# A two-layer decoder trunk on one core: the token order of the group products, the mean of a layer norm, and the last stores

## The chip, the cores and the metric

The kernel runs on 1 core of one Trainium2 chip. The metric is device time in microseconds (us) of that core, the median over several runs. TensorE (PE in the profile; PEld is its weight load) multiplies matrices into PSUM, which has eight banks of 128 partitions x 512 float32 each. VectorE (DVE) and ScalarE (ACT) do the elementwise work, GpSimd (POOL) and SyncE (SP) issue transfers; ACT can issue them too.

## The reference, cut to what matters

All tensors are float32; `x` is (1, 256, 2048): 256 tokens with 2048 features. Layer 0 mixes tokens by pooling, layer 1 by a dilated attention whose keys and values come from the stream behind layer 0; each is followed by a convolutional FFN of inner width 5504, and each of the four sublayers by `layer_norm(alpha * h + mix)`.

```python
def pool_mixer(h, w_in, w_grp, scale, w_out):
    p = (h @ w_in).reshape(B_, S, 4, 512)
    ...                       # pooled: per group a trailing mean over 2, 4, 8 or 16 tokens, minus p
    mixed = jnp.einsum('bsgc,gcd->bsgd', pooled, w_grp).reshape(B_, S, D) * scale
    return mixed @ w_out

def layer_norm(x, g, b):
    mu = jnp.mean(xf, axis=-1, keepdims=True)
    var = jnp.mean(jnp.square(xf - mu), axis=-1, keepdims=True)
    return (xf - mu) * lax.rsqrt(var + 1e-5) * g + b

for i in range(2):
    mix = pool_mixer(...) if i == 0 else dilated_attention(h, h0 @ shared_w_k, h0 @ shared_w_v, ...)
    h = layer_norm(ALPHA * h + mix, ln1_g[i], ln1_b[i])
    h = layer_norm(ALPHA * h + conv_ffn(h, ...), ln2_g[i], ln2_b[i])
```

## The kernel before, in words

**Units.** All weights are read once, in blocks of 512 rows by 512 columns (1 MB), and each block is a unit: it is loaded (`do_load`, line 61, SP's queue, three buffers), split into a high part rounded to PE's float32r format and the rest (`do_split`, lines 86 and 87: `wh` by ACT, then `wl` by DVE, four buffers each), and multiplied. `run_units` (line 105) goes through the units in the order of the list. For unit i it first emits the loads up to i + 5 and the splits up to i + 3 (`ahead`), then the functions put down for this unit in `before`, then the unit's matmuls, then the functions that `later(n, ...)` put off and that are due, then the unit's own evacuation (`post`). This is the order of the instructions on every engine, and each engine works off its own in order. The split of unit i + 3 writes the buffers that unit i - 1 read.

**Operands.** The stream is kept with features on partitions, in "quads": tiles of 128 partitions x 4 blocks x (high, low) x 256 tokens (`quad_tile`, 263). Every product is summed from three: high x high, high weight x low stream, low weight x high stream. `mm_quad` (147) makes such a unit with the weights as the held operand and the tokens as the moving one: 16 pairs of a row block k and a column block m. In mode "ab" a pair is a matmul of 512 columns (L186) and one of 256 (L188); in modes "a", "x" and "grp" it is three of 256 or 258 (L190, L191, L192). In a group's last unit m is the outer loop. The tokens are moved through PE by `cols` (159). The usual order is `twine` (129): the two halves of the 256 tokens in turn (token 0, token 128, token 1, ...); `untwine` and `phi` (132, 141) read a bank back. Four banks hold the results of a group of units (`group`, 197).

**Token order.** From the first layer's residual on, the stream keeps the 128 tokens of a half in another order, j-major with token = 4k + j (j = 0 to 3, k = 0 to 31). The input product and the pooling work in natural order. The new order comes in at the four group products (`add_grp`, 543, mode "grp", one unit each): there `cols` reads `pooled` as `p j k a`, so the results come out in the new order. `grp_post` (505) scales them and writes `mixed`, high part by ACT (L511), low part by DVE (L512). Units of the first layer: the input product for group 3, then group 2, the group product of 3, input 1, group product 2, input 0, group product 1, two units of the output product, group product 0, the other fourteen. An input group is four units, and its evacuation (`pool_post`, 474) does the pooling on DVE; its last step, `lo_part` (L267), ends `pooled`.

**The mean.** `chain` (395) makes the layer norm of a finished residual: PE sums the stream and its squares over the features into one bank (`ps[0]`, L399), the mean in columns 0 to 255 and the mean square behind it. L404 squares the mean (ACT), L405 subtracts (DVE), `root` takes the root (L408, ACT), its reciprocal (L409) and mean times reciprocal (L410, both DVE). It is called three times. With `which` 0 (both first norms) `root` follows at once. With `which` 1 (the end of layer 0) it is put off to the next unit, behind that unit's split. What follows, over the next units: `norm` (L420, L421), `affine` (L427, L429: the high part `xc`) and `lo` (L267: the low part). PE meanwhile works on the unnormalised stream `xp` (mode "x"): behind layer 0 on the first key group (4 units) and the first query group (4 units). The value product (`group_tm`, 215, with `tm_block`, 206, L211 to L213) then reads `xc`; there the tokens are held, a unit is 24 matmuls of 512 columns, and the third of them is the first to read the low part.

**The end.** The last down projection works by token rows, so the last norm goes by rows of 128 tokens (t = 0, t = 1). `finish_second` (807) writes the last four column blocks with L832, in the order 0, 1, 3, 2, and calls `store` (748) behind each: four transfers of 32 partitions x 2 KB, as the tokens' order asks. For t = 1 they go in turn to SP and ACT.

Of the kernel before, what the change touches and what calls it, by code (L numbers as in the profile page):

```python
# [9 lines left out]
F32 = mybir.dt.float32  # L10
F32R = mybir.dt.float32r
I32 = mybir.dt.int32
AF = mybir.ActivationFunctionType
OP = mybir.AluOpType
# [3 lines left out]
T = 256  # L18
# [15 lines left out]
def trunk(ctx: ExitStack, tc: tile.TileContext, x, pool_w_in, pool_w_grp, pool_scale, pool_w_out,  # L34
          attn_w_q, attn_w_o, shared_w_k, shared_w_v, ffn_w_up, ffn_conv_w, ffn_conv_b, ffn_w_down,
          ln1_g, ln1_b, ln2_g, ln2_b, out):
    nc = tc.nc
    V, A, PE = nc.vector, nc.scalar, nc.tensor
# [10 lines left out]
    def bank(nm):  # L49
        return psp.tile([P, 512], F32, name=nm, tag="ps")  # L50
# [22 lines left out]
    def do_split(i, n=4):  # L73
        if i not in parts:
            r = raw.pop(i)
            shape = [P, r.shape[1], r.shape[2]]
            if i < len(units) - 2:
                wh[i] = wp.tile(shape, F32R, name=f"wh{i}", tag="wh")
                wl[i] = wp.tile(shape, F32R, name=f"wl{i}", tag="wl")
            else:  # L80
                for w, nm in ((wh, "wxh"), (wl, "wxl")):
                    v = quad_tile(nm).rearrange("p k l c -> p (k l c)")[:, :shape[1] * shape[2]]
                    w[i] = v.rearrange("p (k n) -> p k n", n=shape[2])
            parts[i] = [(r[:, s], wh[i][:, s], wl[i][:, s]) for s in pieces(i, r.shape[1])]
        for r, h, l in parts[i][:n]:
            A.copy(h, r)  # L86
            V.tensor_tensor(l, r, h.bitcast(F32), OP.subtract)  # L87
        parts[i] = parts[i][n:]
# [40 lines left out]
    def twine(w):  # L129
        return w.rearrange("p (a c) -> p c a", a=2)  # L130

    def untwine(ps):
        return ps.rearrange("p (c a) -> p a c", a=2)

    def apart2(v):
        return v.rearrange("p (a c) -> p a c", a=2)
# [4 lines left out]
    def phi(ps):  # L141
        return untwine(ps[:, :T])
# [4 lines left out]
    def mm_quad(xq, ps, first, last, mode, mid):  # L147
        def go(h, l):
            nk, nb = h.shape[1], h.shape[2] // P
            order = [(k, m) for k in range(nk) for m in range(nb)]  # L150
            if last:
                order = [(k, m) for m in range(nb) for k in range(nk)]
            if first:
                for m in range(nb):
                    ps.append(bank("acc"))
            q = xq()
            n = XW if mode == "x" else T

            def cols(k, j):
                if mode == "grp":  # L160
                    return q[:, k, j, :n].rearrange("p (a k j) -> p j k a", a=2, j=4)
                return twine(q[:, k, j, :n])

            u = state["done"]
            if u < 2:
                for k in range(nk):
                    if k == 3 - u:
                        if u == 0:
                            x_quad(1, (0,))
                            do_split(1, 1)  # L170
                            x_quad(1, (1,))
                            do_split(1, 1)
                        else:
                            mid()
                    for w, j, st in ((h, 0, first and k == 0), (h, 1, False), (l, 0, False)):
                        for m in range(nb):
                            PE.matmul(ps[m][:, :n], w[:, k, m * P:(m + 1) * P], cols(k, j), start=st, stop=False)  # L177
                        if u == 0 and k == 1 and j == 0 and w is h:
                            x_quad(0, (1,))
                            do_split(0, 2)  # L180
                return
            for i, (k, m) in enumerate(order):
                c = slice(m * P, (m + 1) * P)
                st, sp = first and k == 0, last and k == nk - 1
                if mode == "ab":
                    PE.matmul(ps[m], h[:, k, c], q[:, k, :, :T].rearrange("p l (a c) -> p l c a", a=2),  # L186
                              start=st, stop=False)
                    PE.matmul(ps[m][:, :T], l[:, k, c], cols(k, 0), start=False, stop=sp)  # L188
                else:
                    PE.matmul(ps[m][:, :n], h[:, k, c], cols(k, 0), start=st, stop=False)  # L190
                    PE.matmul(ps[m][:, :n], h[:, k, c], cols(k, 1), start=False, stop=False)  # L191
                    PE.matmul(ps[m][:, :n], l[:, k, c], cols(k, 0), start=False, stop=sp)  # L192
                if mid is not None and i == 7:
                    mid()
        return go

    def group(w, r0s, c0, ncol, xqs, post, mode="ab", mids=()):
        ps = []
        for j, (r0, nr) in enumerate(r0s):
            last = j == len(r0s) - 1  # L200
            units.append((w[r0:r0 + nr, c0:c0 + ncol],
                          mm_quad(xqs[j], ps, j == 0, last, mode, mids[j] if j < len(mids) else None),
                          (lambda: post(ps)) if last else None))
# [59 lines left out]
    def quad_tile(nm):  # L263
        return xcp.tile([P, 4, 2, XW], F32R, name=nm, tag="xc")
# [130 lines left out]
    def chain(ps, lay, which, after):  # L395
        mean, msq = ps[:, :T], ps[:, T:]
        for o, v in ((mean, ST["S"]), (msq, ST["Q"])):
            for i in range(2):
                PE.matmul(o, invr, v[:, i], start=i == 0, stop=i == 1)  # L399
        t2 = lnp.tile([P, 2, T], F32, name="var", tag="fold2")  # L400
        rm = lnp.tile([P, 4, T], F32, name="rm", tag="sq")[:, 0:2]
        rs, mr = rm[:, 0:1, :], rm[:, 1:2, :]
        ST["rs"], ST["mr"] = rm[:, 0, :], rm[:, 1, :]
        A.activation(t2[:, 0, :], mean, AF.Square)  # L404
        V.tensor_tensor(t2[:, 1, :], msq, t2[:, 0, :], OP.subtract)  # L405

        def root():
            A.activation(t2[:, 1, :], t2[:, 1, :], AF.Sqrt, bias=epst)  # L408
            V.reciprocal(rm[:, 0, :], t2[:, 1, :])  # L409
            V.tensor_tensor(rm[:, 1, :], mean, rm[:, 0, :], OP.mult)  # L410

        if which == 0:
            root()
        else:
            before.setdefault(state["done"] + 1, []).append(root)
        mb, rb = mr.to_broadcast([P, 4, T]), rs.to_broadcast([P, 4, T])
        g0 = 32 * which

        def norm(q):
            V.tensor_tensor(H[q], H[q], rb, OP.mult)  # L420
            V.tensor_tensor(H[q], H[q], mb, OP.subtract)  # L421

        def affine(q):
            XC[q] = quad_tile("xc")
            for m in range(4):
                j = 4 * q + m
                A.activation(H[q][:, m, :], H[q][:, m, :], AF.Identity,  # L427
                             scale=vec[lay][:, g0 + j:g0 + j + 1], bias=vec[lay][:, g0 + 16 + j:g0 + 17 + j])
            A.copy(XC[q][:, :, 0, :T], H[q])  # L429

        def lo(q):
            lo_part(XC[q], H[q], 4)
            if after is not None:
                later((8, 11, 14, 19)[q], lambda: after(q))

        later(1, lambda: norm(0))
        for q in range(4):
            later(2 + q, lambda q=q: affine(q))
            if q < 3:
                later(2 + q, lambda q=q: norm(q + 1))  # L440
            later(3 + q, lambda q=q: lo(q))
# [30 lines left out]
    pooled_q, mixed_q = {}, {}  # L472
# [32 lines left out]
    def grp_post(g):  # L505
        def post(ps):
            mixed_q[g] = t = quad_tile("mixed")
            for m in range(4):
                sc = vec[0][:, 64 + 4 * g + m:65 + 4 * g + m]
                th, tl = apart2(t[:, m, 0, :T]), apart2(t[:, m, 1, :T])  # L510
                A.activation(th, phi(ps[m]), AF.Copy, scale=sc)  # L511
                V.scalar_tensor_tensor(tl, phi(ps[m]), sc, th.bitcast(F32),  # L512
                                       op0=OP.mult, op1=OP.subtract)
        return post

    XIN = {}
# [24 lines left out]
        group(pool_w_in[0], rows4, 512 * g, 512, xsrcs, pool_post(g), mode="ab" if g < 3 else "a", mids=mids)  # L541

    def add_grp(g):
        group(pool_w_grp[0, g], [(0, 512)], 0, 512, [lambda: pooled_q[g]], grp_post(g), mode="grp")

    marks = []
    add_in(3, mids=[None] + [lambda q=q: x_quad(q) for q in (2, 3)])
# [1 line left out]
    add_grp(3)  # L549
    add_in(1)  # L550
    add_grp(2)
    add_in(0)
    add_grp(1)
# [194 lines left out]
    def store(c, t):  # L748
        rows = out[0, t * P:(t + 1) * P, 512 * c:512 * c + 512].rearrange("(k j) c -> j k c", j=4)
        for j in range(4):  # L750
            queue = A if t == 1 and j % 2 == 1 else nc.sync
            queue.dma_start(rows[j], HT[c][32 * j:32 * j + 32, t, :])

    def tm_post(c, first, last, back=False):
# [85 lines left out]
    scale = 1.0 / math.sqrt(P)  # L840
# [162 lines left out]
    with tc.tile_pool(name="pool", bufs=1) as pp:  # L1003
# [5 lines left out]
        for l in range(2):  # L1009
            n = 80 if l == 0 else 64  # L1010
# [93 lines left out]
```

## Time and profile before

| what | value |
|---|---|
| median of 3 runs | 1944.86 us (1944.46 to 1946.63) |
| the profiled execution | 1945.11 us, its span 1942.9 us |
| mean granted PE clock | 0.999 |
| PE busy | 99% (10486 matmuls) |
| DVE, ACT, POOL busy | 72%, 51%, 16% |
| DMA | 409.89 MB, 211 GB/s |

The span runs from the first to the last instruction of the profiled execution; launch and end around it are in the execution's own time. A line of the timeline gives the start in us, the duration in us, the engine, the line of the code, the operation, what is written and read, and the count; in brackets stands the engine's idle time in front of it and what ended it. SPq, ACTq and POOLq are the queues on which these engines issue transfers. Matmuls are pipelined: a duration is longer than the distance from one start to the next, and the distance is what the matmul costs.

### The profile page before, as it was taken

How to read it: one execution, taken by the hardware profiler on the slowest of the kernel's cores; microseconds unless marked ns; L12 is line 12 of the kernel's file. 1: busy time of each engine (PE TensorE's matmuls, PEld its weight loads, DVE VectorE, ACT ScalarE, POOL GpSimd, SP SyncE). 2: the span in 40 equal slices, each digit the busy share in tenths (PEclk: the TensorE clock that was granted, in tenths of full speed). 3: DMA queues.
4: the chain of work that ended last, by engine and by line, in shares of the span. 5: the costliest groups of instructions: out<-in, count | busy, mean ns of one | idle time of the engine just before them, and what ended most of it. 6: DMA issues, size and time to landing. Idle time of an engine off the chain costs nothing.

```text
span 1942.9 us, 27350 instructions
## 1 busy us (share of the span) xinstructions
PE 1931.4 (99%) x10486; PEld 1733.4 (89%) x10486; DVE 1408.5 (72%) x1782; ACT 996.0 (51%) x1048; POOL 308.6 (16%) x599
## 2 busy tenths in 40 slices
PE   9999999999999999999999999999999999999998
PEld 9999998888888888999999999998888888888897
DVE  7757987856675676789877657888765675575677
ACT  6444575535543554555654444575544553553562
POOL 2000005502110116100033110003511110100100
PEclk9999999999999999999999999999999999999999
DMA  8644648966766667665575665647876665656655
GB/s 275 202 162 151 217 168 253 266 225 207 248 217 208 230 212 227 208 215 195 169 226 187 197 203 174 203 158 232 259 244 211 233 230 203 222 209 219 206 186 183
DMA packets 226018, 409.89 MB, mean 211 GB/s; under 512 B 20462, under 2 KB 39300, under 8 KB 225632
## 3 DMA queue, kind: packets, MB, share of 16 engines
q1 hardware_dynamic: 206912, 389.85, 60.3%
q0 software_dynamic: 18592, 17.78, 3.8%
q8 instruction: 82, 1.34, 0.3%
q10 hardware_dynamic: 384, 0.52, 0.1%
q14 instruction: 48, 0.39, 0.1%
HBM read 380.01 MB, written 2.10 MB: 197 GB/s over the span
## 4 chain that ended last, share of the span: by engine, by line
PE 97%; DVE 2%; DMA 0%; issue 0%; ACT 0%; SPq 0%; DVEq 0%
PE t L211 20%; PE t L213 20%; PE t L212 20%; PE acc L186 18%; PE acc L188 9%; PE acc L190 3%; PE acc L192 3%; PE acc L191 3%; DVE wl L87 1%; PE acc L177 1%; PE s L894 0%; PE o L953 0%; DVE xp L390 0%; DMA raw<-in_attn_w_q_dram 0%; DMA raw<-in_pool_w_in_dram 0%; DVE fold L329 0%
## 5 line engine op out<-in xcount | busy, mean ns | idle before, releaser
L87 DVE TENSOR_TENSOR wl<-raw,wh 128x2048 fp32r<-128x2048 f32 (+2 forms) x374 | 815.1, 2185 | 443.3 <-ACT wh L86 436.4
L86 ACT CAST wh<-raw 128x2048 fp32r<-128x2048 f32 (+2 forms) x374 | 679.8, 1824 | 639.6 <-PE t L213 372.2
L211 PE MATMUL t<-wh,xc 128*128 128x512 f32 x1184 | 449.6, 380 | 0.0
L212 PE MATMUL t<-wl,xc 128*128 128x512 f32 x1184 | 448.7, 379 | 0.0
L213 PE MATMUL t<-wh,xc 128*128 128x512 f32 x1184 | 448.7, 379 | 0.0
L186 PE MATMUL acc<-xc,wh 128*128 128x512 f32 x960 | 317.6, 384 | 0.0
L613 POOL DMA_DIRECT2D u<-b x264 | 130.0, 500 | 1127.8 <-DVE b L604 719.1
L188 PE MATMUL acc<-xc,wl 128*128 128x256 f32 x960 | 261.2, 272 | 0.0
L213 PEld LDWEIGHTS t<-wh,xc 128*128 128x128 f32 x1184 | 223.8, 189 | 31.8
L211 PEld LDWEIGHTS t<-wh,xc 128*128 128x128 f32 x1184 | 223.8, 189 | 31.7
L212 PEld LDWEIGHTS t<-wl,xc 128*128 128x128 f32 x1184 | 223.8, 189 | 31.6
L211 PE MATMUL t<-wh,g 128*128 128x512 f32 x590 | 222.8, 378 | 0.0
L212 PE MATMUL t<-wl,g 128*128 128x512 f32 x590 | 222.8, 378 | 0.0
L213 PE MATMUL t<-wh,g 128*128 128x512 f32 x590 | 222.8, 378 | 0.0
L186 PEld LDWEIGHTS acc<-xc,wh 128*128 128x128 f32 x960 | 180.6, 188 | 26.7 <-ACT h L537 0.6
L188 PEld LDWEIGHTS acc<-xc,wl 128*128 128x128 f32 x960 | 184.3, 192 | 0.4
L629 DVE SCALAR_TENSOR_TENSOR c<-u,cv,c 128x256 f32<-128x256 f32 x344 | 141.2, 479 | 5.9 <-ACT c L625 5.4
L211 PEld LDWEIGHTS t<-wh,g 128*128 128x128 f32 x590 | 111.5, 189 | 15.7
L213 PEld LDWEIGHTS t<-wh,g 128*128 128x128 f32 x590 | 111.5, 189 | 15.6
L212 PEld LDWEIGHTS t<-wl,g 128*128 128x128 f32 x590 | 111.5, 189 | 15.6
L190 PE MATMUL acc<-xp,wh 128*128 128x258 f32 x384 | 106.5, 277 | 4.2 <-DVE rm L410 4.2
L191 PE MATMUL acc<-xp,wh 128*128 128x258 f32 x384 | 106.4, 277 | 0.0
(222 smaller groups left out, 2348.5 us busy)
## 6 DMA issues: line engine op xcount, KB each, us to landing
raw<-in_ffn_w_up_dram SPq DMA_DIRECT2D x160, 1024.0 KB, 5.0
raw<-in_ffn_w_down_dram SPq DMA_DIRECT2D x80, 1024.0 KB, 5.6
raw<-in_pool_w_out_dram SPq DMA_DIRECT2D x16, 1024.0 KB, 5.1
raw<-in_shared_w_k_dram SPq DMA_DIRECT2D x16, 1024.0 KB, 5.2
raw<-in_attn_w_q_dram SPq DMA_DIRECT2D x16, 1024.0 KB, 5.3
raw<-in_shared_w_v_dram SPq DMA_DIRECT2D x16, 1024.0 KB, 5.7
raw<-in_attn_w_o_dram SPq DMA_DIRECT2D x16, 1024.0 KB, 5.2
raw<-in_pool_w_in_dram SPq DMA_DIRECT2D x12, 1024.0 KB, 5.8
```

Of the source, the lines that this page charges most:

```text
L86: A.copy(h, r)
L87: V.tensor_tensor(l, r, h.bitcast(F32), OP.subtract)
L186: PE.matmul(ps[m], h[:, k, c], q[:, k, :, :T].rearrange("p l (a c) -> p l c a", a=2), start=st, stop=False)
L188: PE.matmul(ps[m][:, :T], l[:, k, c], cols(k, 0), start=False, stop=sp)
L190: PE.matmul(ps[m][:, :n], h[:, k, c], cols(k, 0), start=st, stop=False)
L191: PE.matmul(ps[m][:, :n], h[:, k, c], cols(k, 1), start=False, stop=False)
L192: PE.matmul(ps[m][:, :n], l[:, k, c], cols(k, 0), start=False, stop=sp)
L211: PE.matmul(ps, xh, hk, start=first and k == 0, stop=False)
L212: PE.matmul(ps, xh, lk, start=False, stop=False)
L213: PE.matmul(ps, xl, hk, start=False, stop=last and k == nk - 1)
L613: queue.dma_start(w[32 * i:32 * i + 32, 2 + j, :], v[32 * j:32 * j + 32, i, :])
L629: V.scalar_tensor_tensor(c[:, :, m], u[:, i:i + 4, m], cv[:, i, j:j + 1], c[:, :, m], op0=OP.mult, op1=OP.add)
```

## The change

The moving operand of the group products is now `twine`, as elsewhere (their mode is "a"), so their results come out in natural order, and the new order is taken in the evacuation: ACT and DVE read the bank as `p a j k`, whose innermost step is eight floats, and write `mixed` in one run. DVE does each column block in two instructions, one for each half of the tokens. In `chain`, ACT copies the mean into the tile that will hold mean times reciprocal, and `root` multiplies there in place, so that L405 and this copy are the last readers of the bank. The last stores (t = 1) go to SP, SP or ACT by block, ACT, and GpSimd; those of t = 0 stay on SP.

```diff
--- before.py
+++ after.py
@@ -157,8 +157,6 @@
             n = XW if mode == "x" else T
 
             def cols(k, j):
-                if mode == "grp":
-                    return q[:, k, j, :n].rearrange("p (a k j) -> p j k a", a=2, j=4)
                 return twine(q[:, k, j, :n])
 
             u = state["done"]
@@ -402,12 +400,13 @@
         rs, mr = rm[:, 0:1, :], rm[:, 1:2, :]
         ST["rs"], ST["mr"] = rm[:, 0, :], rm[:, 1, :]
         A.activation(t2[:, 0, :], mean, AF.Square)
+        A.copy(rm[:, 1, :], mean)
         V.tensor_tensor(t2[:, 1, :], msq, t2[:, 0, :], OP.subtract)
 
         def root():
             A.activation(t2[:, 1, :], t2[:, 1, :], AF.Sqrt, bias=epst)
             V.reciprocal(rm[:, 0, :], t2[:, 1, :])
-            V.tensor_tensor(rm[:, 1, :], mean, rm[:, 0, :], OP.mult)
+            V.tensor_tensor(rm[:, 1, :], rm[:, 1, :], rm[:, 0, :], OP.mult)
 
         if which == 0:
             root()
@@ -507,10 +506,12 @@
             mixed_q[g] = t = quad_tile("mixed")
             for m in range(4):
                 sc = vec[0][:, 64 + 4 * g + m:65 + 4 * g + m]
-                th, tl = apart2(t[:, m, 0, :T]), apart2(t[:, m, 1, :T])
-                A.activation(th, phi(ps[m]), AF.Copy, scale=sc)
-                V.scalar_tensor_tensor(tl, phi(ps[m]), sc, th.bitcast(F32),
-                                       op0=OP.mult, op1=OP.subtract)
+                th, tl = (apart2(t[:, m, i, :T]).rearrange("p a (j k) -> p a j k", j=4) for i in range(2))
+                src = phi(ps[m]).rearrange("p a (k j) -> p a j k", j=4)
+                A.activation(th, src, AF.Copy, scale=sc)
+                for a in range(2):
+                    V.scalar_tensor_tensor(tl[:, a], src[:, a], sc, th[:, a].bitcast(F32),
+                                           op0=OP.mult, op1=OP.subtract)
         return post
 
     XIN = {}
@@ -541,7 +542,7 @@
         group(pool_w_in[0], rows4, 512 * g, 512, xsrcs, pool_post(g), mode="ab" if g < 3 else "a", mids=mids)
 
     def add_grp(g):
-        group(pool_w_grp[0, g], [(0, 512)], 0, 512, [lambda: pooled_q[g]], grp_post(g), mode="grp")
+        group(pool_w_grp[0, g], [(0, 512)], 0, 512, [lambda: pooled_q[g]], grp_post(g), mode="a")
 
     marks = []
     add_in(3, mids=[None] + [lambda q=q: x_quad(q) for q in (2, 3)])
@@ -748,7 +749,7 @@
     def store(c, t):
         rows = out[0, t * P:(t + 1) * P, 512 * c:512 * c + 512].rearrange("(k j) c -> j k c", j=4)
         for j in range(4):
-            queue = A if t == 1 and j % 2 == 1 else nc.sync
+            queue = nc.sync if t == 0 else (nc.sync, (nc.sync, A, A, nc.sync)[c], A, nc.gpsimd)[j]
             queue.dma_start(rows[j], HT[c][32 * j:32 * j + 32, t, :])
 
     def tm_post(c, first, last, back=False):
```

## The prediction

> **What bounds the kernel now.** I read the page first: its busy table, the chain that ended last, then the waits of TensorE (PE), and only then single stretches of the timeline.
>
> ```profile
> span 1942.9 us, 27350 instructions
> PE 1931.4 (99%) x10486; PEld 1733.4 (89%) x10486; DVE 1408.5 (72%) x1782; ACT 996.0 (51%) x1048; POOL 308.6 (16%) x599
> ```
>
> The longest wait of PE (us in total, times, longest; the next two in that view are of the warm-up, before 10 us, and about a microsecond each):
>
> ```profile
> PE acc L190 <- DVE rm L410: 4.2, 1, 4.2
> ```
>
> PE is busy for 99% of the span and waits once for long. So three things can change the end: how long PE needs for its matmuls, that one wait of 4.2 us, and the tail behind PE's last matmul. Each part of the change touches one of them. The profiled execution took 1945.11 us, of which 2.2 lie around the span; the median of the three runs is 1944.86, 0.25 less. I sum against the execution and carry the differences over to the median.
>
> **Part 1, the group products.** A busy PE says nothing about its pace, so I looked at starts. The four units that read `pooled` have 48 matmuls each. Starts and durations, for the first and the last of the four: its first matmul, then the first one behind it; in between stands the start of the second group unit, four ordinary units later:
>
> ```profile
> 54.55 0.39 PE L190 MATMUL acc<-pooled,wh 128*128 128x256 f32 x1
> ...
> 65.53 0.40 PE L186 MATMUL acc<-xc,wh 128*128 128x512 f32 x1
> ...
> 86.50 0.40 PE L190 MATMUL acc<-pooled,wh 128*128 128x256 f32 x1
> ...
> 139.92 0.40 PE L190 MATMUL acc<-pooled,wh 128*128 128x256 f32 x1
> ...
> 150.89 0.40 PE L186 MATMUL acc<-mixed,wh 128*128 128x512 f32 x1
> ```
>
> 10.98 and 10.97 us, 0.229 us a matmul; an ordinary unit takes (86.50 - 65.53) / 4 = 5.24. The new operand has the form of the `g` units of the last column block of layer 0's down projection: same 256 columns, same three matmuls, two halves in turn, one element a step. There are 132 of them:
>
> ```profile
> 881.72 0.28 PE L190 MATMUL acc<-g,wh 128*128 128x256 f32 x1
> ...
> 896.46 0.28 PE L190 MATMUL acc<-xp,wh 128*128 128x258 f32 x1
> ```
>
> 14.74 us / 132 = 0.1117 us. So the old operand, which walks tokens in steps of four (16 bytes), runs at half the pace. A unit becomes 48 x 0.1117 = 5.36 us, and four of them save 4 x (10.98 - 5.36) = **22.5 us** of PE time.
>
> Does PE get that time, or does it then wait? What lies around the first group unit, on VectorE (DVE):
>
> ```profile
> 54.79 2.29 DVE L87 TENSOR_TENSOR wl<-raw,wh 128x2048 fp32r<-128x2048 f32 x1 [1.72 <-ACT wh L86]
> ...
> 63.81 2.28 DVE L87 TENSOR_TENSOR wl<-raw,wh 128x2048 fp32r<-128x2048 f32 x1
> 66.02 1.22 DVE L267 TENSOR_TENSOR pooled<-po,pooled 128x1024 fp32r<-128x1024 f32 x1
> 67.15 1.66 DVE L512 SCALAR_TENSOR_TENSOR mixed<-acc,vec,mixed 128x256 fp32r<-128x256 f32 x4
> 68.72 2.28 DVE L87 TENSOR_TENSOR wl<-raw,wh 128x2048 fp32r<-128x2048 f32 x1
> ```
>
> Counted off in the program, these three splits are of the second, third and fourth unit behind the group unit. It will now end at 59.9, and those three start at 65.1, 70.4 and 75.6. Their splits end at 57.1, 66.1 and about 71.7 (below), a slack of 8, 4.3 and 3.9 us. The next group unit is due at 80.9; its operand, `pooled` above, is done at 67.2. The later groups are looser: there DVE idles ahead of most splits, because ACT waits for PE to free a weight buffer. Over the whole stage:
>
> ```profile
> 54.50:151.00 96.50, 96.50 (x515) 88.03 (x514) 60.03 (x60) 39.60 (x45) 0.00 (x0) 1.00 0.52 174
> ```
>
> DVE has 60.0 us of work in 96.5; with 22.5 less it has 60 to 62 in 74, 84%, and DMA stands at 0.52. PE stays the bound.
>
> The evacuation now reads the bank in steps of eight floats (32 bytes) and DVE does it in two halves. Nothing in the trace reads a bank so; the nearest rows are two ScalarE (ACT) copies of 512 columns, contiguous (L534) and in runs whose step is four floats (L537):
>
> ```profile
> L534 ACT CAST xc<-xT x7: 586/586/597, 4.7 to 23.8; 128x512 fp32r<-128x512 f32 x7
> L537 ACT COPY h<-xT x8: 581/604/618, 15.2 to 32.7; 128x512 f32<-128x512 f32 x8
> L512 DVE SCALAR_TENSOR_TENSOR mixed<-acc,vec,mixed x16: 475/478/485, 67.2 to 151.6; 128x256 fp32r<-128x256 f32 x16
> 972.33 0.28 DVE L910 SCALAR_TENSOR_TENSOR p<-p,cnt 128x128 f32<-128x128 f32 x1
> ```
>
> 604 against 586 ns: a step costs ACT 3% at most. Half the columns take DVE 0.28 us, so a pair 0.56 for 0.478; a group's evacuation grows by 4 x 0.08 = 0.3 us, or 0.7 at 0.33 a half. All of it lies in the slack of 3.9 us, so I cost it at nothing; between nothing and twice the old price (1.9 us a group) the sum is the same. From the other side: the Trainium skill's "SBUF — State Buffer", section "Door 1: The DMA port swizzle", says that PSUM has lines of 8 bytes and that any non-contiguous PSUM access slows matmuls significantly. It speaks of matmuls, and ACT's row at 16 bytes does not show it; whether it holds for DVE at 32 no row tells. I make it a rival below.
>
> **Part 2, the mean.** The one wait of PE, the row before it, and the clock after it (window: length, then busy us of PE, PEld, DVE, ACT, POOL, PE clock, DMA share, GB/s):
>
> ```profile
> 919.28 0.27 PE L192 MATMUL acc<-xp,wl 128*128 128x258 f32 x1
> 923.75 0.58 PE L190 MATMUL acc<-xp,wh 128*128 128x258 f32 x1 [4.20 <-DVE rm L410]
> ```
>
> ```profile
> 923.75:929.70 5.95, 5.95 (x40) 5.95 (x41) 5.88 (x5) 3.12 (x5) 0.00 (x0) 0.74 0.48 153
> ```
>
> PE should have gone on at 919.39, so it lost 4.36 us, and then ran at a mean clock of 0.74 for 5.95 us, 1.55 us more: 5.9 in all. What it waited for is the bank that holds the mean, of which L410 is the last reader:
>
> ```profile
> 917.08 0.42 DVE L405 TENSOR_TENSOR var<-acc,var 128x256 f32<-128x256 f32 x1
> 919.29 2.29 DVE L87 TENSOR_TENSOR wl<-raw,wh 128x2048 fp32r<-128x2048 f32 x1 [1.79 <-ACT wh L86]
> ...
> 923.28 0.42 DVE L410 TENSOR_TENSOR rm<-acc,rm 128x256 f32<-128x256 f32 x1
> ```
>
> With the copy the bank is free after L405, at 917.5, 1.9 us before PE needs it. The copy is at most 0.6 us of ACT (L537 above moves twice the columns in 0.604) in front of this:
>
> ```profile
> 917.35 1.90 ACT L86 CAST wh<-raw 128x2048 fp32r<-128x2048 f32 x1 [3.56 <-DMA raw<-in_attn_w_q_dram]
> ```
>
> ACT idles 3.56 us there, so the copy is free. Behind the copy are queued only the splits and the root. In the two other chains (near 235 and 1272) the root follows at once; ACT waits for L405 between square and root anyway, so the copy fits in, and no PE wait is there to be removed.
>
> What is late next? The chain of root, norm and affine on DVE and ACT stays, since it hangs on the weights that land at 917.35. PE will come earlier to the value product, which reads the new stream:
>
> ```profile
> 945.75 0.38 PE L211 MATMUL t<-wh,xc 128*128 128x512 f32 x1
> ...
> 946.18 0.38 PE L213 MATMUL t<-wh,xc 128*128 128x512 f32 x1
> ```
>
> ```profile
> 937.49 1.22 DVE L267 TENSOR_TENSOR xc<-h,xc 128x1024 fp32r<-128x1024 f32 x1
> ...
> 945.29 1.22 DVE L267 TENSOR_TENSOR xc<-h,xc 128x1024 fp32r<-128x1024 f32 x1
> ...
> 951.03 1.22 DVE L267 TENSOR_TENSOR xc<-h,xc 128x1024 fp32r<-128x1024 f32 x1
> ```
>
> ```profile
> 929.76 1.91 ACT L86 CAST wh<-raw 128x2048 fp32r<-128x2048 f32 x1 [0.48 <-PE acc L191]
> ```
>
> Two starts in 0.43 us are 0.215 us a matmul, 24 x 0.215 = 5.16 us a unit. Without the stall the product starts at 945.75 - 5.9 = 939.85. It needs the low parts of quads 0, 1, 2 from the third matmul (0.43 us) of each unit. DVE and ACT gain only the 0.48 us that ACT waits for PE at 929.76, so the low parts end at 938.2, 946.0 and 951.75. Quad 0 is in time; quad 1 is wanted at 945.44 and costs 0.6; quad 2 is then wanted at 951.2 and costs 0.5. So 1.1 of the 5.9 come back as small waits and **4.8 us** stay; 4.3 if DVE and ACT don't move at all, 5.9 if they move more.
>
> **Part 3, the last stores.** The last result of DVE, the last issues, the wait in front of them, and issues and landings by queue:
>
> ```profile
> 1937.43 0.74 DVE L832 SCALAR_TENSOR_TENSOR ht<-ht,mv,w 128x512 f32<-128x512 f32 x1
> ```
>
> ```profile
> 1939.23 0.82 SPq L752 DMA_DIRECT2D out_dram<-ht  x2
> 1939.45 0.79 ACTq L752 DMA_DIRECT2D out_dram<-ht  x2
> ```
>
> ```profile
> SPq L752 <- DMA out_dram<-ht: 0.4, 1, 0.4
> ```
>
> ```profile
> u<-b POOLq DMA_DIRECT2D x264, 32.0 KB, 2.0
> ...
> ht<-hb POOLq DMA_DIRECT2D x128, 32.0 KB, 6.2
> ...
> out_dram<-ht ACTq DMA_DIRECT2D x8, 64.0 KB, 2.0
> ```
>
> The result is there at 1938.17, the last issue ends at 1940.24: eight stores on each of two queues at 0.40 us, and a wait for an earlier store in front of the last pair. With 6, 6 and 4 the issues alone would end near 1939.0 (two on ACT after 1938.17); but a last one that still waits for the landing of the fourth, issued near 1936.9 (DVE's second result of four) and down 2.0 us later, starts at 1938.9 and ends at 1939.3. That is 0.9 us; I take **0.8**. Bounds: 1.2 gained if nothing waits, and 2.5 lost if GpSimd's last store takes the 6.2 us of `ht<-hb` (1938.2 + 6.2 = 1944.4; now the last store goes at 1939.85 and lands 2.0 later, at 1941.9). I sit near the gain, since a store of whole rows is like `u<-b`, not like the scattered `ht<-hb`. GpSimd has no other work in the tail.
>
> **Sum.** 22.5 + 4.8 + 0.8 = 28.1 us. 1944.86 - 28.1 = 1916.8 (the profiled execution: 1917.0).
>
> **The rivals.**
> (a) The freed bank gains nothing because PE then waits as long for something else in the same place. For it: DVE is busy 5.88 of 5.95 us there, and the stream comes through DVE. Against it: the low part of quad 1 is at most 1.1 us late as worked out. Time: 22.5 + 0.8, so 1921.6. Chance 0.12.
> (b) DVE becomes the bound in the group stage. For it: DVE is busy without a break from 54.8 to 71, and the slack is 3.9 us. Against it: the 84% above. If each group gives back 1.2 us: 1921.6. Chance 0.05.
> (c) The change of operand doesn't speed the matmuls, because the slow pace hangs on something else than the step of the read. For it: only that no other unit reads `pooled`. Against it: tile shape, type and column count are those of `g`. Time: 1944.86 - 5.6 = 1939.3. Chance 0.03.
> (d) Slower: reading a bank in steps of 32 bytes makes the evacuation so long that the split queued behind it comes too late. It has to eat the 3.9 us of slack, then 7 us more a group to cancel the sum, then 1 more to be seen: 12 us over eight halves, 1.5 us on top of 0.28, more than six times the price. At eight times it is 8 x 1.96 - 3.9 = 11.8 us a group, 47 in all, 1963.6. Against it: the 3% of L537. Chance 0.02. (It is the rule of the Trainium skill's "SBUF — State Buffer" above, taken to hold for DVE's reads.)
>
> **How the numbers follow.** The forecast has 0.78. Range: the best ends (22.9 + 5.9 + 1.2 = 30.0) give 1914.9, and the three runs lie 2.2 us apart, so 1913.8; upward it takes in rivals (a) and (b) at 1921.6 and 1 us more for the tail, 1922.6. A measurement of this kernel tells some 0.2% (3.9 us) from no change. Every case but (d) is faster by more: 0.97; slower 0.02; 0.01 between.
>
> **What would show it.** Group units of 5.4 us starting 48 x 0.112; no wait of PE for `rm`, clock 1.00 behind 918 minus the shift; instead waits under 1 us for `xc` at the value product; DVE halves of about 0.3 us; last issue some 1.2 us behind DVE's last result. Halves of over 1.5 us, a PE wait for `wl` behind a group unit, or group matmuls still 0.229 apart would prove me wrong.

## The result, and the profile after

The changed kernel takes 1918.63 us (median of four runs, 1918.2 to 1921.32) against 1945.58 for the kernel before on the same chip (four runs, 1944.46 to 1946.63): a ratio of 0.9864 [0.9847, 0.9882]. The profiled execution took 1918.88 us, 26.2 less than the profiled one of before. The page:

```profile
span 1917.1 us, 27384 instructions
PE 1907.3 (99%) x10486; PEld 1714.1 (89%) x10486; DVE 1409.3 (74%) x1798; ACT 996.2 (52%) x1051; POOL 309.5 (16%) x603
```

PE has the same 10486 matmuls and is busy for 24 us less; the other engines do the work they did. PE's waits, in the form shown of before (total, times, longest):

```profile
PE warm L993 <- DVE epst L995: 1.1, 1, 1.1
PE o L954 <- DMA pTl<-pB: 1.0, 1, 1.0
PE acc L175 <- ACT wh L86: 0.7, 1, 0.7
PE t L211 <- DVE xc L265: 0.3, 1, 0.3
```

The wait of 4.2 us for `rm` is gone. A wait for `pTl`, the transposed attention weights of the second two heads of a group of four, has come in; it stood nowhere in the prediction.

Since the matmuls are the same and in the same order, the n-th start of after can be set against the n-th of before. The difference changes in these places only:

| place | PE comes earlier by (us) |
|---|---|
| up to 54 us, ahead of any change | 0.7 |
| the four group units | 22.5 |
| the mean's bank (wait 4.4, slow clock behind it 1.5) | 5.9 |
| the value product, two small waits | -0.3 and -0.55 |
| the attention outputs `o`, near 990 us | -1.3 |
| last matmul to the end of the execution | -0.74 |

The first row is no part of the change: the code up to there is the same. 0.5 of it comes between 32 and 34 us, where three matmuls of 512 columns took 0.48 us each before and 0.38 after. The first 10 us can differ by more: in `group_and_mean` below, eight matmuls of 256 columns take 2.08 us from 6.27 on, in before 1.16 us from 6.37 on, and PE is 1.7 us later at 10 us. The runs of before lie near 1944.5 or near 1946.5, with a few between; what makes that, no kept trace shows.

**The groups.** First start of the first group unit, and of the unit behind it, on PE:

```profile
53.89 0.28 PE L188 MATMUL acc<-pooled,wh 128*128 128x256 f32 x1
59.25 0.38 PE L184 MATMUL acc<-xc,wh 128*128 128x512 f32 x1
```

5.36 us for 48 matmuls is 0.1117 each, and a matmul now lasts 0.28 us where it lasted 0.39 to 0.41. DVE behind that unit, and the evacuation's groups of instructions (count; min/median/max ns; first and last start):

```profile
62.73 2.28 DVE L87 TENSOR_TENSOR wl<-raw,wh 128x2048 fp32r<-128x2048 f32 x1
64.93 1.22 DVE L265 TENSOR_TENSOR pooled<-po,pooled 128x1024 fp32r<-128x1024 f32 x1
66.07 2.15 DVE L513 SCALAR_TENSOR_TENSOR mixed<-acc,vec,mixed 128x128 fp32r<-128x128 f32 x8
68.14 4.48 DVE L87 TENSOR_TENSOR wl<-raw,wh 128x2048 fp32r<-128x2048 f32 x2
```

```profile
L511 ACT ACTIVATE mixed<-acc,vec x16: 461/472/488, 63.8 to 127.9; 128x256 fp32r<-128x256 f32 x16
```

```profile
L513 DVE SCALAR_TENSOR_TENSOR mixed<-acc,vec,mixed x32: 340/342/352, 66.1 to 128.7; 128x128 fp32r<-128x128 f32 x32
```

A group's eight halves take DVE 2.15 us (1.66 before with four whole ones), ACT's reads of the bank in steps of eight floats 472 ns (474 before, in steps of two floats). The splits queued behind them start at 68.14, and PE waits for no `wl` in this stage.

**The mean.** The last readers of the bank, and what now comes late, on DVE; then PE where the bank was waited for:

```profile
893.89 0.42 DVE L404 TENSOR_TENSOR var<-acc,var 128x256 f32<-128x256 f32 x1
896.03 2.29 DVE L87 TENSOR_TENSOR wl<-raw,wh 128x2048 fp32r<-128x2048 f32 x1 [1.72 <-ACT wh L86]
...
900.02 0.42 DVE L409 TENSOR_TENSOR rm<-rm 128x256 f32<-128x256 f32 x1
```

```profile
896.22 0.28 PE L188 MATMUL acc<-xp,wh 128*128 128x258 f32 x1
```

```profile
896.00:902.00 6.00, 6.00 (x56) 6.00 (x55) 5.90 (x5) 2.31 (x2) 0.00 (x0) 1.00 0.89 321
```

The bank is free at 894.31, 1.91 us before PE's 896.22; the root's last step still comes at 900.02, but PE no longer hangs on it, and the clock stays at 1.00. Most of the price comes 94 us later:

```profile
990.44 0.46 PE L954 MATMUL o<-pTl,vt 128*128 128x256 f32 x1 [1.03 <-DMA pTl<-pB]
```

**The tail.** Rows of the drains behind an engine's last work, POOL's and SP's (three values: shortest, median, longest in ns; then the first and the last start), after:

```profile
L1100 POOLq DRAIN  x3: 46/102/4567, 1911.8 to 1916.8; - x3
L1100 SPq DRAIN  x3: 7/7/7, 1915.0 to 1916.6; - x3
```

and before:

```profile
L1099 POOLq DRAIN  x3: 46/102/4759, 1850.0 to 1942.6; - x3
```

Both kernels have one long drain of GpSimd, at its last DMA issue. Before, that issue was a transfer of the last convolution (`u<-b`) at 1850.4, and the drain of 4.8 us, from 1850.0, was over 88 us ahead of the end, where it cost nothing. GpSimd now issues stores at the end, and its drain of 4.6 us lies there: from 1911.75 to 1916.32, past SP's first drain at 1915.0. From the end of PE's last matmul to the end of the span it takes 6.69 us, where it took 5.48.

### The profile page after: what moved, and what is told of

Read it like the earlier page. It is cut to its first block, busy times and chain, and to the rows that moved or that the text cites. A ratio compares the mean times of both kernels' runs of the same rounds, so it can differ in the third digit from the quotient of the medians.

```text
span 1917.1 us, 27384 instructions
## 1 busy us (share of the span) xinstructions
PE 1907.3 (99%) x10486; PEld 1714.1 (89%) x10486; DVE 1409.3 (74%) x1798; ACT 996.2 (52%) x1051; POOL 309.5 (16%) x603
## 4 chain that ended last, share of the span: by engine, by line
PE 90%; issue 5%; DVE 3%; DMA 1%; ACT 1%; POOL 0%; SPq 0%; DVEq 0%; POOLq 0%; ACTq 0%
PE t L211 19%; PE t L209 19%; PE t L210 19%; PE acc L184 17%; PE acc L186 8%; PE acc L190 2%; PE acc L188 2%; PE acc L189 2%; DVE wl L87 1%; DMA pTl<-pB 1%; PE acc L175 1%; PE s L895 0%; PE o L954 0%; ACT wh L86 0%; DVE xp L388 0%
```

## The experiments

My theory after the result: the groups' 22.5 us hang on the step of the moving operand; the bank's 5.9 us hang on its last reader, and about 2 us of them come back at the next things that PE has to wait for; the stores lose where they were to gain, through GpSimd's drain, which they move to the end. Rivals are named with the runs.

**Part 1 alone** (`group_alone`: the copy and the queues as before). The rival has DVE as the new bound, so that the groups gain less by themselves than beside the other parts.

```diff
-        A.copy(rm[:, 1, :], mean)
...
-            V.tensor_tensor(rm[:, 1, :], rm[:, 1, :], rm[:, 0, :], OP.mult)
+            V.tensor_tensor(rm[:, 1, :], mean, rm[:, 0, :], OP.mult)
...
-            queue = nc.sync if t == 0 else (nc.sync, (nc.sync, A, A, nc.sync)[c], A, nc.gpsimd)[j]
+            queue = A if t == 1 and j % 2 == 1 else nc.sync
```

> Only the group products take the new operand and the new evacuation; mean and stores stay as before. My theory (each group unit costs 48 distances between matmuls, and PE is the bound there): four units of 5.37 us instead of 10.98, so 22.5 us less than the kernel before, and PE still waits 4.2 us once for the product of mean and reciprocal (L410). Rival (VectorE becomes the bound of the stage): group units as short, but PE waits for wl behind them, and under 18 us are gained.

Measured: 1922.6 us (1922.16 to 1923.68), ratio 0.9885 [0.987, 0.99], 22.2 below the 1944.78 of the kernel before in that set. The units take 5.36 us, and the old wait stands untouched:

```profile
PE acc L188 <- DVE rm L408: 4.1, 1, 4.1
```

The whole of the 22.5 arrives. The rival falls.

**Part 2 alone** (`mean_alone`: the kernel before with the copy). The rival: the give-back is only the two small waits at the value product, so that 4.8 stay.

```diff
         A.activation(t2[:, 0, :], mean, AF.Square)
+        A.copy(rm[:, 1, :], mean)
...
-            V.tensor_tensor(rm[:, 1, :], mean, rm[:, 0, :], OP.mult)
+            V.tensor_tensor(rm[:, 1, :], rm[:, 1, :], rm[:, 0, :], OP.mult)
```

> Only the mean is copied out of its bank; group products and stores stay as before. My theory: the wait of 4.2 us and the half clock behind it go (5.9 us by the two traces), and about 2.0 come back: 0.7 at the value product for the low parts of xc, 1.3 at the attention outputs (o), which come to wait for the transposing DMAs into pTl. Net 3.9 us less than before. Rival of the prediction: 1.1 come back, at the value product alone, net 4.8. Other rival: another wait of the same size takes its place, net 0.

Measured: 1940.11 us (eight runs, 1939.51 to 1940.48), ratio 0.9974 [0.9964, 0.9985], 4.7 less. PE's waits:

```profile
PE o L954 <- DMA pTl<-pB: 0.5, 1, 0.5
PE t L213 <- DVE xc L267: 0.3, 1, 0.3
```

By the starts of the matmuls it gains 5.92 and gives back 0.30 and 0.55 at the value product and 0.77 at `o`, 1.6 in all; 4.3 stay. Both numbers, 4.7 by the medians and 4.3 by the starts, lie between the two theories, and the median alone would not have told them apart; the wait for `pTl` does: it comes with the mean's part, without the groups.

**Part 3 alone** (`stores_alone`: the kernel before with the new queues). Rival: the prediction's, 0.8 faster.

```diff
-            queue = A if t == 1 and j % 2 == 1 else nc.sync
+            queue = nc.sync if t == 0 else (nc.sync, (nc.sync, A, A, nc.sync)[c], A, nc.gpsimd)[j]
```

> Only the last stores are put on three queues. My theory from the two traces: the last stores land about as long after VectorE's last result (3.5 us) as before, since the 16 of them together are bound by what the DMA engines move, and GpSimd then spends about 4.3 us in a drain that begins with its last issue and outlasts everything else by 1.3 us. From the end of PE's last matmul to the end of the span: 6.7 us instead of 5.5, the time 1.2 longer. Rival (the prediction): the last landing comes 0.8 us earlier and the time is 0.8 shorter.

Measured: 1946.4 us (ten runs, 1945.19 to 1947.5), ratio 1.0005 [0.9995, 1.0014]. The time does not tell it from no change. The trace does: from the last matmul to the end of the span 6.76 us against 5.48, with the same long drain:

```profile
L1099 POOLq DRAIN  x3: 46/102/4634, 1939.5 to 1944.6; - x3
```

Of these 1.28 us 0.46 come back around the span (the execution is 1.78 us longer than its span, 2.24 before), so about 0.8 are lost. The gain of 0.8 is not there.

**Parts 1 and 2, stores as before** (`group_and_mean`).

```diff
-            queue = nc.sync if t == 0 else (nc.sync, (nc.sync, A, A, nc.sync)[c], A, nc.gpsimd)[j]
+            queue = A if t == 1 and j % 2 == 1 else nc.sync
```

> Group products and mean as changed, the stores on two queues as before. My theory: the tail is the old one (5.5 us from PE's last matmul to the end), no drain of GpSimd at the end, 1.2 us of span less than the changed kernel (1917.1), so 1915.9. Rival (three queues do help): about 0.8 us of span more than the changed kernel, 1917.9.

Measured: 1918.33 us (1917.64 to 1919.52), ratio 0.9863 [0.9848, 0.9877], 26.4 below its 1944.78. The median is too near that of the changed kernel, 1918.63 on another chip, to tell the stores. Its tail does: it is 5.58 us, and POOL's long drain is back at GpSimd's last transfer of the convolution, at 1824.3:

```profile
L1100 POOLq DRAIN  x3: 46/102/4337, 1824.3 to 1917.0; - x3
```

Its profiled execution had lost 1.7 us against before in the first 10 us, so its own span says nothing on the stores.

**A store for GpSimd, but early** (`gpsimd_one_store`: GpSimd issues one store of the first column block, the others of its four go to SP). If the drain is a fixed time behind GpSimd's last issue, it ends before the other stores and costs nothing; if GpSimd's stores are slow themselves, the tail stays long.

```diff
-            queue = nc.sync if t == 0 else (nc.sync, (nc.sync, A, A, nc.sync)[c], A, nc.gpsimd)[j]
+            queue = nc.sync if t == 0 else (nc.sync, (nc.sync, A, A, nc.sync)[c], A, nc.gpsimd if c == 0 else nc.sync)[j]
```

> The changed kernel, but GpSimd issues one of the last 16 stores only, the last one of the first column block; its three others go to SP. My theory (GpSimd's drain begins with its last issue and takes 4.3 us, or ends 1.9 us after its last landing): it ends before SP has seen the last landing, and from the end of PE's last matmul to the end of the span it is 5.5 us, as before the change. Rival: GpSimd's drain waits for all transfers of the tail or costs its 1.3 us whenever GpSimd has a store there, so 6.7 us.

Measured, a single run: 1917.65 us.

```profile
L1100 POOLq DRAIN  x3: 46/102/4037, 1908.5 to 1915.3; - x3
L1100 SPq DRAIN  x3: 7/7/7, 1914.7 to 1915.0; - x3
```

The drain lasts 4.04 us behind one single store and is over at 1912.5, ahead of SP's. So it is a time of its own, hidden here as it was before the change. The tail is 6.36 us and not the 5.5 that I had set: SP has nine of the sixteen stores, its last issue ends 2.75 us behind DVE's last result, and the last landing is 4.05 us behind it. That part of my expectation fell: one queue with too many stores lengthens the tail as well. (A late semaphore of GpSimd's in the closing steps, at 1915.68, is a further 0.3 of it.) The time itself, 1 us below the changed kernel's, is mostly not the stores': PE lost 0.5 us at `o` and not 1.3, and the tail gave 0.3. So that the drain alone makes the changed kernel's 1.2 us is read from the order of its trace, where the closing steps start 0.2 us behind the drain's end; no run keeps GpSimd's four stores and hides the drain.

**The copy made, but not used** (`copy_unused`: `root` reads the bank again). Rival to the last reader: that the copy, or ACT's new order, moved something else.

```diff
-            V.tensor_tensor(rm[:, 1, :], rm[:, 1, :], rm[:, 0, :], OP.mult)
+            V.tensor_tensor(rm[:, 1, :], mean, rm[:, 0, :], OP.mult)
```

> The changed kernel, but the product of mean and reciprocal reads the mean from its bank again; ScalarE's copy is made and not used. My theory (PE waited for the bank, whose last reader is that product): the wait of about 4.2 us on it and the half clock behind it are back, the waits at the value product and at pTl are gone, and the copy itself costs nothing. Rival: the wait was ended by the copy's effect on the order of the engines, and stays away.

Measured, a single run: 1925.53 us, and

```profile
PE acc L188 <- DVE rm L409: 4.1, 1, 4.1
```

The wait is back, and the waits at the value product and at `o` are gone. Behind the wait PE ran at a clock of 0.50 for 5.3 us, where before it was 3.1 (the row has the form of the prediction's windows):

```profile
902.29:907.60 5.31, 5.31 (x24) 5.31 (x25) 5.28 (x4) 2.91 (x5) 0.00 (x0) 0.50 0.42 164
```

Its span is 6.6 us longer than the changed kernel's: 1.8 of it was lost in the first 55 us, ahead of the edit; 4.25 is the wait and 2.6 the slow clock behind it; 2.1 is what no longer is given back. The cause is the last reader of the bank and nothing else; the copy itself costs nothing that can be seen. The slow clock also says what the bank is worth: wait and clock together cost 5.9 us in before, 6.0 in `group_alone`, 6.9 here and 7.0 in `stores_alone`.

**The second transposition one unit earlier** (`turn_one_unit_earlier`). DVE transposes the second half of the attention weights (L929 before, L930 after) 18 to 19 us after the first, and GpSimd issues the transfers that bring it to `pTl`:

```profile
997.19 0.97 DVE L929 STREAM_TRANSPOSE pB<-p 128x768 f32<-128x768 f32 x1
```

```profile
971.80 0.97 DVE L930 STREAM_TRANSPOSE pB<-p 128x768 f32<-128x768 f32 x1
```

The first of these two rows is of before, the second of after: DVE came 25.4 us earlier, PE 28.3. The last of those transfers landed at 1013.14 before, 4.4 us ahead of PE's 1017.5; after, at 989.98, where PE wanted it at about 989.2. If the transposition's place is what is late, a unit earlier takes the wait away and gives about 1.3 us; if the transfers are held up by others, the wait stays.

```diff
-                    later(n + 8, lambda: turn(hq, (2, 3)))
+                    later(n + 7, lambda: turn(hq, (2, 3)))
```

> The changed kernel, but the second turning of the attention weights of each head quad (VectorE's transposes and GpSimd's 16 DMAs into pTl) is put one unit earlier. My theory (PE waits 1.0 us near 990 because these DMAs moved only with VectorE while PE moved further): the wait on pTl is gone, nothing else appears, and the span is about 1.3 us shorter behind that place. Rival: the turning then stands ahead of a split that PE needs, or finds the attention weights not ready, and PE waits there as long for wl or o.

Measured, a single run: 1917.5 us. The wait for `pTl` is gone, with 1.27 us by the starts of the matmuls, and no new one has come:

```profile
PE warm L993 <- DVE epst L995: 1.1, 1, 1.1
PE acc L175 <- ACT wh L86: 0.5, 2, 0.3
PE t L211 <- DVE xc L265: 0.3, 1, 0.3
```

**Which step is slow** (`four_steps`: the four group products read `pooled` in steps of 1, 2, 4 and 8 floats, for groups 0 to 3, without the two halves in turn; the evacuation puts the order right). My theory had the step of 4 as too far and 2 floats as near enough. The Trainium skill's "SBUF — State Buffer", section "Door 1: The DMA port swizzle", says so too: a read has full bandwidth as long as it hits each line of 16 bytes twice or more. Rivals: the pace falls further with the step, or not at all (it hung on something else).

```diff
+STEPS = (1, 2, 4, 8)
...
             def cols(k, j):
+                if mode.startswith("s"):
+                    return q[:, k, j, :n].rearrange("p (m s) -> p s m", s=int(mode[1:]))
...
```

> The changed kernel, but each group product reads its tokens with another step: group 0 one float apart (4 bytes), group 1 two (8), group 2 four (16), group 3 eight (32), all in one run of the two halves; each evacuation undoes its order. My theory (the pace hangs on how many neighbouring floats of a 16-byte stretch are read close together; the Trainium skill's page SBUF - State Buffer, section Door 1, says that two of the four are enough): steps of 4 and 8 bytes run at 0.112 us a matmul, steps of 16 and 32 bytes at 0.229. Rival: the pace is set by the number of nested steps of the operand or by switching between the halves, so that all four (one or two nested steps, no switching) run at 0.112. Other rival: the pace falls with the step, 0.112, 0.15, 0.229, 0.45.

Measured, a single run: 1937.08 us. First starts of the first unit (8 floats) and of the last (1 float), and the unit behind the last:

```profile
55.74 0.38 PE L191 MATMUL acc<-pooled,wh 128*128 128x256 f32 x1
...
140.81 0.28 PE L191 MATMUL acc<-pooled,wh 128*128 128x256 f32 x1
...
146.53 0.38 PE L187 MATMUL acc<-mixed,wh 128*128 128x512 f32 x1
```

| step | 1 float | 2 floats | 4 floats | 8 floats |
|---|---|---|---|---|
| unit, us | 5.72 | 11.0 | 11.15 | 10.46 |
| a matmul, us | 0.119 | 0.229 | 0.232 | 0.218 |

Two floats are as slow as four, and eight are no slower. The rivals fall, and so does the half of my theory that is on two floats. The Trainium skill's rule does not hold for the moving operand here: a step of 8 bytes hits every line of 16 twice and runs at half the pace all the same (0.229 us).

**What is fast, then** (`pairs_and_streams`: group 3 reads pairs of neighbouring floats, 16 bytes apart; groups 2, 1, 0 read 4, 8 and 16 parts of the row in turn, one float each). Theory: a read is fast when each 8 bytes are used whole within two floats, or from a few rows in turn.

```diff
+MODES = ("w16", "w8", "w4", "pairs")
...
             def cols(k, j):
+                if mode == "pairs":
+                    return q[:, k, j, :n].rearrange("p (m s b) -> p s m b", s=2, b=2)
+                if mode.startswith("w"):
+                    return q[:, k, j, :n].rearrange("p (a c) -> p c a", a=int(mode[1:]))
...
```

> The changed kernel with another order of reading in each group product, each undone in its evacuation (which needs more instructions for that, 2 to 8 times as many): group 3 takes pairs of neighbouring floats, the pairs 16 bytes apart (floats 0 1, 4 5, ...); groups 2, 1, 0 go through 4, 8 and 16 parts of the row in turn, one float further at each round. My theory after the run with four steps (8 bytes apart ran at 0.229: what counts is that both floats of an 8-byte pair are read, near each other): pairs at about 0.112 to 0.12, four parts in turn at 0.112 still, and somewhere between 4 and 16 parts the two reads of a pair lie too far apart and the pace drops to 0.229. Rival (only a row read without gaps, or two such rows in turn, is fast): pairs at 0.229, and all of 4, 8 and 16 at 0.229. Other rival (distance between the two reads of a pair doesn't matter): 4, 8, 16 all at 0.112.

Measured, a single run (for 16 parts without one gap of 0.68 us in the unit, with which it is 0.231):

| read | two halves in turn (after) | 4 parts | 8 parts | 16 parts | pairs |
|---|---|---|---|---|---|
| a matmul, us | 0.1117 | 0.140 | 0.223 | 0.221 | 0.229 |

The pairs fall out of the theory: whole 8 bytes do not make it fast. What both runs leave is a description: full pace, or nearly, for a row read in one run without gaps or in two in turn, a quarter more for four in turn, half the pace for everything else that was tried. The mechanism stays open.

This kernel took 1975.96 us, 31 more than the kernel before, since its evacuation has two to eight times as many DVE instructions as the changed kernel's:

```profile
PE acc L189 <- DVE mixed L529: 31.5, 4, 8.0
```

Four waits of about 8 us for `mixed`, during and behind which the clock was at half for 34 us: the way to lose that the prediction's rival (d) named, an evacuation too long for its slack, does exist, at a price that the change does not come near.

**The best of it** (`mean_group_turn`: parts 1 and 2, the stores as before, the transposition a unit earlier), beside the changed kernel again (`changed_again`).

```diff
-            queue = nc.sync if t == 0 else (nc.sync, (nc.sync, A, A, nc.sync)[c], A, nc.gpsimd)[j]
+            queue = A if t == 1 and j % 2 == 1 else nc.sync
...
-                    later(n + 8, lambda: turn(hq, (2, 3)))
+                    later(n + 7, lambda: turn(hq, (2, 3)))
```

> Group products and mean as changed, the last stores on two queues as before, and the second turning of the attention weights one unit earlier. My theory (the parts add up: 22.5 for the groups, 5.9 for the bank, 0.7 back at the value product, nothing back at pTl, the old tail): 27.7 us less than the kernel before, so about 1917.1 where that one has 1944.8, and 1 to 2 us less than the changed kernel in the same call. Rival (the parts hide each other, or the turning costs elsewhere): not less than the changed kernel.

> The changed kernel once more, beside the combined version and the kernel before on the same chip: 26 to 27 us less than before; its profile shows the drain of GpSimd behind the last issue (4.3 us) and the wait for pTl (0.3 to 1.0 us) again.

Measured: 1917.12 us (1916.97 to 1917.18), ratio 0.9857 [0.9842, 0.9871], against 1918.47 (1918.29 to 1918.69), ratio 0.9864 [0.9847, 0.988]. All four runs of the one lie below all four of the other, by 1.35 us in the median. Its waits, without `pTl`:

```profile
PE acc L175 <- ACT wh L86: 1.3, 2, 0.8
PE warm L993 <- DVE epst L995: 1.1, 1, 1.1
PE t L211 <- DVE xc L265: 0.3, 1, 0.3
```

The tail is 5.52 us where the changed kernel's is 6.73; with what lies around the span (2.2 against 1.8 us) that is 0.8. The wait for `pTl`, 0.8 by the starts, is the other part; against them go 0.3 us that this execution lost ahead of 54 us.

## Why the prediction was right, and which terms were not

**Groups: 22.5 forecast, 22.50 measured.** The step was to price the new operand by units of the same form (`g`) and not by PE's busy share, and 0.1117 us came out to the digit. That the cause is the order of the read was argued there and is shown by `four_steps`, where tile, type and column count stay and the pace goes with the order; but "steps of four" names only the case, since a step of two floats, or pairs with gaps, is as slow. DVE's slack held: halves of 0.342 us were a little above the 0.28 to 0.33 assumed, and a group's 0.5 us more vanished in it.

**A bank read in steps of 32 bytes.** The prediction weighed a rule of the Trainium skill ("SBUF — State Buffer", section "Door 1: The DMA port swizzle") against ACT's row. For ACT the row was right (472 ns after, 474 before). For DVE the halves cost 0.342 us where the prediction had 0.28 from L910, which does not read a bank at all: its inputs lie in SBUF. The same instruction with 128 columns stands in `four_steps` for the group read in steps of four floats, whose evacuation reads the bank in runs of 32 floats without gaps:

```profile
L530 DVE SCALAR_TENSOR_TENSOR mixed<-acc,vec,mixed x8: 341/351/353, 99.0 to 102.9; 128x128 fp32r<-128x128 f32 x8
```

That is no faster than 342 ns in steps of eight floats. So the step cost DVE nothing, and the 0.5 us a group come from cutting each read in two.

**Mean: 4.8 forecast, 3.8 measured.** The gross 5.9 was right, and the bank was free 1.91 us ahead of PE as worked out. The small waits at the value product were 0.8 and not 1.1. The step that failed is "what is late next": it ended at the value product, and the next thing that hangs on DVE's order rather than on PE's, the second transposition with GpSimd's transfers behind it, cost 1.3. It had 4.4 us of slack; PE moved by 28.3 and that chain's last landing by 23.2 only, which makes it 0.7 late, and PE starts 0.46 us behind the landing (989.98 to 990.44). The 5.1 between them are 2.9 of DVE's order, which moved by 25.4, and 2.2 of the transfers themselves: from GpSimd's last issue to the last landing it took 5.6 us and 3.4 before. Without that second part PE would have been in time; what slowed the transfers stays open, and the run with the earlier transposition shows only that a unit more of slack is enough. The 1.3 is also the largest of its kind: in the six other traces with this part of the change and the transposition in its old place, the same place cost 0.2 to 0.8.

**Stores: 0.8 faster forecast, 0.74 slower measured.** Two steps failed. The first is that fewer issues a queue end the tail earlier. The last issue did come earlier, 1.47 us behind DVE's last result and not 2.07:

```profile
1909.80 1.40 DVE L833 SCALAR_TENSOR_TENSOR ht<-ht,mv,w 128x512 f32<-128x512 f32 x2
```

```profile
1911.49 0.50 POOL L753 DMA_DIRECT2D out_dram<-ht  x1 [0.17 <-issue]
...
1911.85 0.31 SPq L753 DMA_DIRECT2D out_dram<-ht  x1
...
1911.98 0.69 ACTq L753 DMA_DIRECT2D out_dram<-ht  x1
```

But the last landing stayed where it was, 3.62 us behind that result (1914.82) against 3.48 before: sixteen stores of 64 KB took 5.69 us from first issue to last landing, 5.54 before. In the three us from 1911 on the DMA engines were busy for 0.95, 1.00 and 0.89 of the time (0.95, 0.82 and 0.83 from 1938 on before), and the stores waited longer there (up to 3.0 us from issue to landing, 2.4 in `group_and_mean`). So I read what had looked like issues as the DMA engines' time to move 1 MB; no run moved less to test it. The second is the drain: the prediction asked only how long GpSimd's transfers take, and put nothing for what follows its last issue, though the row of before, 4759 ns at 1850.0 us, showed it. The bound of 2.5 lost did hold it, but for another reason, a slow landing, which did not come (no store took over 3.0 us).

**Sum.** 22.5 + 3.8 - 0.74 + 0.66 of the start = 26.2, the difference of the two executions. The 0.66 is luck: without it the parts give 25.6 of the 28.1 forecast, with both misses to the same side. Of the rivals, (a) has a grain in it: 2.1 of the 5.9 us of the freed bank (1.6 in `mean_alone`) came back as other waits, not all. Two figures of the prediction are loose, and change no chance: the 22.9 of its range has no row, and rival (d) comes to 1963.8 by its own terms, not 1963.6.

## What to carry to other kernels

A busy PE hides its pace: divide a unit's length by its matmuls and compare units of another operand form, because a gather in the moving operand can halve the pace, while the same gather in the evacuation's read of PSUM cost ACT nothing and DVE a second instruction that its slack hid. When a wait of PE goes, follow every chain that DVE's or GpSimd's order leads, to the end of the stage and not only to the next product, and set its slack against the time that PE gains on it. In a tail, ask first whether issues or the moving of the bytes ends it; and before GpSimd gets a late store, look for the drain behind its last DMA issue, which the store takes to the end with it.

## What the runs showed of the hardware

- Moving operand, float32r, 256 columns: 0.1117 us for two halves in turn, 0.119 for one contiguous row, 0.140 for four parts, 0.22 to 0.23 for every other read tried: steps of 8, 16 or 32 bytes, eight or sixteen parts in turn, pairs with gaps. That two in turn are 6% faster than one row I had not expected, nor that nothing is worse than half.
- At GpSimd's last DMA issue stands one drain of 4.0 to 4.8 us, wherever in the program that is: 4759 ns at 1850.0 us before and 4337 at 1824.3 in `group_and_mean`, hidden; 4567, 4634 and 4037 ns where the last issue was a store near the end. Its other drains last 102 ns at most, but for one of 0.2 us at the start.
- A DVE read of 128 columns of a bank, with the same instruction, took 341 to 353 ns without gaps and 340 to 352 in steps of eight floats.
- A stall of PE costs more than its length: the wait of 4.2 us was followed by 3.1 us at a clock of 0.50 before, which cost another 1.5 us, and that of 4.1 by 5.3 us at 0.50 in `copy_unused`, which cost 2.6.
